# The planner of a two-layer diffusion transformer on one core: matmul durations refitted, and a resource shared by DVE and GpSimd added

## The chip, the cores and the metric

The kernel runs on one core of one Trainium2 chip. The metric is the time on the device, in microseconds (us), of one execution of the whole program; the median of three runs before the change is 2145.59 us. The engines are called as the profile calls them: PE multiplies matrices (PEld is its loading of weights), DVE, ACT and POOL are the vector, scalar and GpSimd engines, and SP issues the DMAs.

## The reference

Two layers work on 256 latent tokens and 256 context tokens of 1024 features. Each layer is a half-step FFN, a token mixer (retention beside latent attention) and a second half-step FFN; a modulation by a condition vector goes ahead of each.

```
mod = (silu_c @ w_ada[l] + b_ada[l])[:, None, :]
mod_c = (silu_cc @ w_ada[l] + b_ada[l])[None, None, :]
...
x = x + 0.5 * g1 * swiglu(modulate(rmsnorm(x), sh1, sc1), ffn1_w1[l], ffn1_w3[l], ffn1_w2[l])
xc = xc + 0.5 * cg1 * swiglu(modulate(rmsnorm(xc), csh1, csc1), ffn1_w1[l], ffn1_w3[l], ffn1_w2[l])
o_lat, o_ctx = token_mixer(...)
x = x + g2 * o_lat
x = x + 0.5 * g3 * swiglu(modulate(rmsnorm(x), sh3, sc3), ffn2_w1[l], ffn2_w3[l], ffn2_w2[l])
```

Here `modulate(h, shift, scale)` is `h * (1 + scale) + shift` and `swiglu` is `(silu(h @ w1) * (h @ w3)) @ w2`. Retention multiplies queries and keys of 8 heads, weights the scores by a decay, multiplies them by the values, normalises each head's output by its mean and variance, and gates it by `silu(g_raw)`. The context has no output in the second layer.

## The kernel before

All features lie on partitions, so each activation is 8 tiles of 128 x 512 (256 latent and 256 context tokens). A matrix product in full precision is made of three products of rounded parts: a value is the sum of a rounded part `hi` and the rest `lo`, and PE does hi by hi, lo by hi and hi by lo (`mm3`). ACT casts a chunk of weights to `wh`, and DVE subtracts it from the raw chunk to get `wl`. For the retention's queries and keys ACT and DVE cast and DVE and POOL subtract (`ret_split`).

The kernel doesn't fix the order of the instructions by hand. The program first records every instruction with the tiles that it reads and writes as a node of a `Plan`. `Plan.order()` then plays through the nodes: each engine takes, of those nodes whose inputs it believes to be ready, the one with the lowest place in the program, corrected by `ahead(n)` for urgent ones. How long a node lasts comes from the table in `Engine.cost()`; how long another engine needs to see its end comes from `LAG`. Tiles have a limited number of slots by kind (51 of `t`, 14 of `u`, 4 each of `raw`, `wh` and `wl`, and 4 each of `m` and `a` in PSUM), and a node with a new tile waits for a slot. `emit()` then issues the instructions in the order found, on the engines' queues. On the chip each engine follows its queue strictly in that order, and waits where an input or a slot is late. All instructions but those of SP are on line 363 for that reason (line 368 in the changed kernel), so tiles tell them apart, not lines.

Three stages matter here. They are called by their stretch of the span.

- The start (0 to 80 us, function `start`). Feature tile by feature tile (k = 0 to 7) the kernel makes the first modulation. For k = 4 to 7 DVE multiplies a row block of the modulation's weights with the row of c and sums it (`junk`, two for each k); POOL makes the same products for the context's row (into `wl`), and ACT sums them. Two tiny instructions (`mod`, 128x2) follow, then the hidden input `H[k]` for each half of the tokens: DVE's `u`, ACT's rounded part, DVE's rest. PE multiplies it with two parts of the first FFN's weights of 128x384, i = 0 and i = 1, that ACT and DVE split as well (`t<-t,t` 128x384): for each k six groups of three products of 512 columns, nine products with i = 0 and nine with i = 1. `ada_stage` and `hidden` are recorded `ahead(URGENT)`, `split` and the products aren't.
- Retention of layer 0 (about 605 to 700 us): `ret_split`, `masks`, `ret_scores` (`a<-t,t` 128x256), `ret_av`, the normalising, and beside them the products of the gates, `g_step` (`m<-t,wh` and `m<-t,wl`, 24 products of 512 columns for each chunk), which need nothing of retention.
- Retention of layer 1 (about 1780 to 1850 us), the same for 256 tokens.

Of the kernel before, what the change touches and what calls it, by code (L numbers as in the profile page):

```python
# [13 lines left out]
F32R = mybir.dt.float32r  # L14
# [4 lines left out]
P = 128  # L19
# [9 lines left out]
# quadrant of a head's rotary rows, and of its unused rows, by head % 4  # L29
# [31 lines left out]
class Halves:  # L61
    """Columns that lie in tiles of their own."""
# [10 lines left out]
class Buffer:  # L73
    """A tile in one of the slots of its kind, from its first instruction to its last one."""
# [15 lines left out]
class View:  # L90
    """A part of a buffer; taken of the tile itself when the instruction is emitted."""
# [23 lines left out]
    def rearrange(self, pattern, **sizes):  # L115
        """Splits and permutes the dimensions after the first."""
# [43 lines left out]
class Node:  # L160
    """Instructions that follow one another on one engine."""

    __slots__ = ("calls", "engine", "cost", "table", "prio", "index", "waits", "after", "bufs", "new", "ready", "start", "end")

    def __init__(self, engine, prio, index):
        self.engine, self.prio, self.index = engine, prio, index
        self.calls, self.cost, self.table = [], 0.0, None
        self.waits, self.after, self.bufs, self.new = set(), [], {}, []
        self.ready, self.start, self.end = 0.0, None, None


class Plan:
    """Takes instructions in the order of the program, and emits them in the order in which engines
    that always take the first of those that are ready would start them."""

    # about how many ns an engine sees it after another is through with an instruction
# [4 lines left out]
    # until when the tensor engine runs at half its speed  # L181
# [13 lines left out]
    @contextmanager  # L195
    def together(self):
        """The instructions of one engine in here are not parted."""
        self.block = False
        yield
        self.block = None  # L200

    @contextmanager
    def ahead(self, n):
        """The instructions in here go before others of up to n places earlier."""
        self.shift += n
        yield
        self.shift -= n

    @contextmanager
    def behind(self, node):  # L210
        """The instructions in here wait for that one."""
        self.held.append(node)
        yield
        self.held.pop()

    def add(self, engine, call, args, kwargs, writes, reads, cost, table):
# [10 lines left out]
        node.table = table  # L227
        for v in reads + writes:
            b = v.buf
            node.waits.update(n for w, n in b.wrote if w.overlaps(v))  # L230
            if b.kind in ("m", "a") and b.wrote:
                # a bank's products come in order, and no reading while there are more to come
# [15 lines left out]
    def order(self):  # L248
# [8 lines left out]
        # free slots, and the indices at which buffers of a kind not yet there come up  # L257
# [8 lines left out]
        dma, table = 0.0, None  # L266
# [5 lines left out]
        def room(n, now):  # L272
            """None where the node's new buffers have slots; else the kind that lacks, and when to look again."""
# [13 lines left out]
        while len(done) < len(nodes):  # L287
# [16 lines left out]
            if e != "PE" and n.cost > self.LONG:  # L304
                # not a long instruction where a far more urgent one comes shortly
# [21 lines left out]
            else:  # L327
                if n.table not in (None, table):
                    now, table = now + self.TABLE, n.table
                slow = 2.0 if e == "PE" and now < self.COLD else 1.0  # L330
# [22 lines left out]
    def emit(self):  # L353
        resolve = lambda v: v.get() if isinstance(v, View) else v  # noqa: E731
# [12 lines left out]
class Engine:  # L367
    """Records the instructions of one engine."""
# [4 lines left out]
    def __getattr__(self, method):  # L373
        call = getattr(self.real, method)

        def record(*args, **kwargs):
# [5 lines left out]
            # the activation functions of one table, which takes its time to load  # L382
            table = {AF.Silu: 0, AF.Exp: 1, AF.Tanh: 1}.get(args[2]) if method == "activation" else None
            return self.plan.add(self.name, call, args, kwargs, out, reads, self.cost(method, out, reads, kwargs), table)

        return record

    def cost(self, method, out, reads, kwargs):
        """About how many ns the engine is held."""
# [6 lines left out]
        if self.name == "PE":  # L396
# [3 lines left out]
            passes = 1 if reads[0].buf.dt == F32R else 4  # L400
# [18 lines left out]
def kernel(  # L419
# [100 lines left out]
    def decays():  # L520
        act.activation(nlg, decT, AF.Exp)
        dve.tensor_scalar(out=lg, in0=nlg, scalar1=-1.0, scalar2=None, op0=ALU.mult)
        # of the two heads of a tile, and of the keys of the context in both directions
# [80 lines left out]
    class Norm:  # L604
        """Root mean square over features, which lie on partitions."""

        def __init__(self, n_tiles, apart=False):
            """apart: the last tile's squares are not added to the others, but come to the sums by themselves."""
# [20 lines left out]
        def stats(self, a, n):  # L629
            """The sums of tokens a..a + n, tokens on partitions."""  # L630
# [13 lines left out]
        def spread(self, a, n):  # L644
            """1 / rms of these tokens on all partitions."""
# [14 lines left out]
    def make_h(y, pair, l, m_sh, k, a):  # L660
        """pair at a = split of y * (1 + scale) + shift."""
# [8 lines left out]
    def modulated(nrm, H, l, m_sh, a, n):  # L670
        """H at a..a + n = split of x / rms * (1 + scale) + shift."""
# [22 lines left out]
    def ada_steps(l, m):  # L694
        """A part of the modulation, its features on partitions: products with the rows of c and c_ctx, summed along the
        rows, by the vector engine for c, by GpSimd and the scalar engine for c_ctx."""
# [26 lines left out]
    def last_gate():  # L723
        """The modulation's last part, wholly on the tensor engine, for a time when that has little else to do."""
# [57 lines left out]
    def update_x(nrm, l, m_g, m, ps, a, b):  # L782
        """x += gate * ps, over tokens a..b, and what the next norm needs of it."""
# [10 lines left out]
    def tail(Ws, X, ks, nrm, l, m_g, n_tok):  # L794
        """The last feature tiles of a residual update: one half of the tokens, then the other one,
        with the first half's norm amid it."""
# [13 lines left out]
    def staggered(nrm, H, l, m_sh, n_tok, groups):  # L810
        """The first products of a phase, half by half as their input comes in.
        groups: pairs of weights, the number of tokens, and what to do with a half of their products."""
# [35 lines left out]
    def ffn(l, w1, w3, w2, m_sh, m_g, nrm_in, nrm_out, n_tok, n_next, fill, pre=None):  # L848
        """pre: hidden input and gated tiles that are there already."""
# [42 lines left out]
        for pi, (k0, k1) in enumerate(PARTS):  # L892
            if pre and pi == 1:
                step(late_consts)
            # at the start more tiles come first, as the gate takes its time
# [29 lines left out]
    def rope(src, cos, sin, mask):  # L925
        """Returns a, b of which the sum is the rotated src (128 x 256, in SBUF)."""
# [8 lines left out]
    def mixer(l, nrm_in, nrm_out, full):  # L935
# [129 lines left out]
        # retention queries and keys, two heads a tile  # L1065
# [12 lines left out]
        # retention values, tokens on partitions  # L1078
# [124 lines left out]
        # a head's keys as (hi; lo) over all rows, its queries' hi and lo twice each: the whole product in two passes  # L1203
        KS, QS = {}, {}
        # for the latent queries and the context's keys: both directions' decayed queries and states, one over the other
# [258 lines left out]
    def start():  # L1464
# [26 lines left out]
        # the rows of c and c_ctx on all partitions  # L1491
# [228 lines left out]
```

## Time and profile before

| what | value |
|---|---|
| runs | 2144.06, 2145.59, 2147.37 us; median 2145.59 |
| span of the profiled execution | 2143.6 us |
| PE busy | 2111.1 us, 98% of the span |
| DVE, ACT, POOL busy | 1419.2, 752.7 and 169.0 us |

The profiled execution's span is 2.0 us under the median of the runs, so what lies around it is taken as 2.0 us. The end of a matmul is modelled in the profile, so that short gaps on PE hide in its busy time; where PE waits is read from its timeline and its granted clock, not from the 98%.

### The profile page before, as it was taken

What the parts mean: (1) busy time and instruction counts of PE and PEld (TensorE: products, weight loads), DVE (VectorE), ACT (ScalarE), POOL (GpSimd) and SP (SyncE); (2) the same over time, 40 slices, a digit from 0 to 9 for tenths busy, and PEclk for the clock granted to TensorE, in tenths of its full rate; (3) what the DMA queues carried; (4) which work ended last, traced back from release to release, by engine and by line L of the source; (5) the groups of instructions that cost most, each with busy time, mean ns of one, the idle gap of its engine ahead of it and who ended that gap; (6) DMA issues with size and microseconds to landing.
All of it is one profiled execution on the core that took longest, in us unless ns stands there. A gap on an engine that the chain in (4) does not pass through costs nothing.

```text
span 2143.6 us, 29821 instructions
## 1 busy us (share of the span) xinstructions
PE 2111.1 (98%) x11610; PEld 1797.2 (84%) x11610; DVE 1419.2 (66%) x2591; ACT 752.7 (35%) x1240; POOL 169.0 (8%) x180
## 2 busy tenths in 40 slices
PE   8999999999999999999999999999999999999998
PEld 5788888987788888988888898888889878999998
DVE  7898885668679435898865473433347977766665
ACT  4422222466433223422212242222225744444433
POOL 3000000211132000100000010000002112100000
PEclk9999999999999999999999999999999999999999
DMA  8476664322212333467666432333333312574663
GB/s 307 130 213 206 199 194 138 87 84 60 63 58 67 107 119 108 120 205 216 191 197 191 128 111 77 108 98 90 98 96 97 116 60 79 155 261 148 204 186 110
DMA packets 86782, 293.76 MB, mean 137 GB/s; under 512 B 9585, under 2 KB 12785, under 8 KB 86641
## 3 DMA queue, kind: packets, MB, share of 16 engines
q1 hardware_dynamic: 86642, 291.87, 44.7%
q8 instruction: 91, 1.49, 0.3%
q14 instruction: 49, 0.40, 0.1%
HBM read 290.78 MB, written 1.05 MB: 136 GB/s over the span
## 4 chain that ended last, share of the span: by engine, by line
PE 83%; DVE 9%; issue 6%; POOL 1%; ACT 1%; DMA 0%; POOLq 0%; DVEq 0%; ACTq 0%
PE m L363 78%; PE a L363 5%; DVE t L363 5%; DVE u L363 2%; DVE wl L363 1%; DVE s L363 1%; DVE junk L363 1%; POOL s L363 1%; ACT t L363 0%; ACT wh L363 0%; POOL t L363 0%; DMA raw<-in_w1b_dram 0%; ACT u L363 0%; DVE x L363 0%; DVE mod L363 0%
## 5 line engine op out<-in xcount | busy, mean ns | idle before, releaser
L363 PE MATMUL m<-t,wh 128*128 128x512 f32 (+1 forms) x6248 | 1643.0, 350 | 0.7 <-DVE t L363 0.6
L363 PEld LDWEIGHTS m<-t,wh 128*128 128x128 f32 x6248 | 1092.1, 188 | 169.0 <-issue 1.9
L363 PE MATMUL m<-t,wl 128*128 128x512 f32 (+1 forms) x3124 | 1085.7, 349 | 0.0
L363 ACT CAST wh<-raw 128x1024 fp32r<-128x1024 f32 (+1 forms) x398 | 408.9, 1029 | 956.5 <-PE m L363 833.9
L363 DVE TENSOR_TENSOR wl<-raw,wh 128x1024 fp32r<-128x1024 f32 (+1 forms) x398 | 477.0, 1199 | 289.2 <-ACT wh L363 288.5
L363 PEld LDWEIGHTS m<-t,wl 128*128 128x128 f32 x3124 | 588.8, 188 | 80.4
L363 DVE SCALAR_TENSOR_TENSOR junk<-raw,crow 128x1024 f32<-128x1024 f32 x220 | 270.6, 1230 | 39.7 <-DMA raw<-in_w_ada_dram 37.5
L363 DVE SCALAR_TENSOR_TENSOR x<-m,mod,x 128x256 f32<-128x256 f32 x192 | 86.5, 480 | 136.7 <-PE m L363 136.5
L363 ACT ACTIVATE t<-m 128x512 f32<-128x512 f32 (+1 forms) x155 | 79.4, 513 | 238.8 <-PE m L363 235.4
L363 DVE TENSOR_TENSOR t<-t,t 128x512 fp32r<-128x512 f32 (+7 forms) x252 | 150.0, 602 | 3.8 <-ACT t L363 1.1
L363 DVE TENSOR_TENSOR t<-t,m 128x512 f32<-128x512 f32 (+1 forms) x91 | 54.5, 599 | 134.2 <-PE m L363 127.4
L363 POOL TENSOR_TENSOR s<-s,mhalf 128x2 f32<-128x2 f32 (+1 forms) x31 | 34.7, 1124 | 1177.0 <-DVE s L363 1176.8
L363 PE MATMUL a<-t,t 128*64 128x256 f32 (+3 forms) x512 | 89.7, 354 | 10.0 <-DVE t L363 7.8
L363 PE MATMUL m<-wh,t 128*128 128x512 f32 x288 | 91.9, 398 | 0.0
L363 PEld LDWEIGHTS a<-t,t 128*128 128x128 f32 (+1 forms) x512 | 66.6, 177 | 29.8 <-DVE t L363 7.8
L363 PE MATMUL m<-t,t 128*128 128x256 f32 (+1 forms) x480 | 75.9, 310 | 8.9 <-ACT t L363 7.4
L363 PEld LDWEIGHTS m<-t,t 128*128 128x128 f32 x480 | 65.3, 191 | 16.2 <-ACT t L363 8.3
L363 PEld LDWEIGHTS m<-wh,t 128*128 128x128 f32 x288 | 53.3, 188 | 12.8 <-issue 1.2
L363 ACT CAST t<-t 128x512 fp32r<-128x512 f32 (+4 forms) x112 | 55.6, 525 | 12.7 <-DVE t L363 11.9
L363 PE MATMUL m<-wl,t 128*128 128x512 f32 x144 | 57.1, 397 | 0.0
L363 ACT ACTIVATE t<-u,mod 128x256 fp32r<-128x256 f32 x88 | 40.1, 500 | 43.0 <-DVE u L363 42.6
L363 POOL MEMSET t<- 32x512 f32 x32 | 16.3, 528 | 431.5 <-PE m L363 217.5
(109 smaller groups left out, 1077.4 us busy)
## 6 DMA issues: line engine op xcount, KB each, us to landing
raw<-in_w_ada_dram SPq DMA_DIRECT2D x124, 512.0 KB, 4.2
raw<-in_w_m_dram SPq DMA_DIRECT2D x76, 512.0 KB, 3.6
raw<-in_w1b_dram SPq DMA_DIRECT2D x44, 512.0 KB, 3.9
raw<-in_w3b_dram SPq DMA_DIRECT2D x44, 512.0 KB, 3.9
raw<-in_w1a_dram SPq DMA_DIRECT2D x41, 512.0 KB, 3.6
raw<-in_w3a_dram SPq DMA_DIRECT2D x41, 512.0 KB, 3.6
raw<-in_w2a_dram SPq DMA_DIRECT2D x32, 512.0 KB, 3.5
raw<-in_w2b_dram SPq DMA_DIRECT2D x32, 512.0 KB, 4.2
```

What stands on the lines that cost most here:

```text
L363: call(*[resolve(v) for v in args], **{k: resolve(v) for k, v in kwargs.items()})
```

## The change

The change touches only what the planner believes. First, a rounded matmul with 128 rows is now costed at columns / 2.25 + 4.3 ns: 231.9 ns for 512 columns, where it was 216.0, and 118.1 ns for 256, where it was 109.4. Second, a node can hold a `port`: every POOL instruction but a memset, and those DVE instructions without a PSUM operand that read two large operands, or are a copy or a tensor_scalar with more than 8 output columns. In the plan such nodes follow one another, whichever of the two engines they are on. All the other lines of the diff only blank comments.

```diff
@@ class Node
-    __slots__ = ("calls", "engine", "cost", "table", "prio", "index", "waits", "after", "bufs", "new", "ready", "start", "end")
+    __slots__ = ("calls", "engine", "cost", "table", "port", "prio", "index", "waits", "after", "bufs", "new", "ready", "start", "end")
...
@@ Plan.add
+        node.port = node.port or port
...
@@ Plan.order
-        dma, table = 0.0, None
+        dma, table, port = 0.0, None, 0.0
...
+                if n.port:
+
+                    now = max(now, port)
+                    port = now + n.cost
                 slow = 2.0 if e == "PE" and now < self.COLD else 1.0
                 n.end = clock[e] = now + slow * n.cost
...
@@ Engine
+    def port(self, method, out, reads, kwargs):
+
+        if self.name == "POOL":
+            return method != "memset"
+        if self.name != "DVE" or any(v.buf.kind in ("m", "a") for v in out + reads):
+            return False
+        big = [v for v in reads if math.prod(v.shape[1:]) > 1]
+        return len(big) > 1 or (method in ("tensor_copy", "tensor_scalar") and math.prod(out[0].shape[1:]) > 8)
...
@@ Engine.cost
-            passes = 1 if reads[0].buf.dt == F32R else 4
+            single = reads[0].buf.dt == F32R
+            passes = 1 if single else 4
+            if single and rows == P:
+                return cols / 2.25 + 4.3
```

No instruction is added or removed. What differs is the order on the engines' queues and the slots of tiles. Of 2345 nodes of DVE 282 stand three or more places off, of 4396 of PE 261, of 1179 of ACT 64, of 171 of POOL 4, and of SP none.

On DVE at the start, before. The rows are those after the junk sums of k = 5 have begun; `t_557` is the rest of the weights' part i = 1 for k = 4, `u_559`, `u_564` and `t_586` make the hidden input of k = 4 (`x_71`):

```order
L363 SCALAR_TENSOR_TENSOR junk,s_522<-raw_363,crow 128x1024
L363 TENSOR_SCALAR mod_1_94<-s_474,sm 128x2
L363 TENSOR_TENSOR t_557<-t_349,t_520 128x384
L363 SCALAR_TENSOR_TENSOR u_559<-x_71,mod_1_94,u_278 128x256
L363 SCALAR_TENSOR_TENSOR u_564<-x_71,mod_1_94,u_287 128x256
L363 TENSOR_SCALAR mod_0_93<-s_522,sm 128x2
L363 SCALAR_TENSOR_TENSOR junk,s_572<-wh_387,crow 128x1024
L363 SCALAR_TENSOR_TENSOR t_586<-u_559,mod_0_93,t_566 128x256
L363 SCALAR_TENSOR_TENSOR t_586<-u_564,mod_0_93,t_566 128x256
```

And on DVE in the changed order, where `t_654` is that same rest for k = 4, i = 1, and `u_637`, `u_641` and `t_647` make the hidden input of k = 6 (`x_73`):

```order
L368 SCALAR_TENSOR_TENSOR u_637<-x_73,mod_1_94,u_289 128x256
L368 SCALAR_TENSOR_TENSOR u_641<-x_73,mod_1_94,u_295 128x256
L368 SCALAR_TENSOR_TENSOR junk,s_589<-wh_422,crow 128x1024
L368 SCALAR_TENSOR_TENSOR t_647<-u_637,mod_0_93,t_644 128x256
L368 SCALAR_TENSOR_TENSOR t_647<-u_641,mod_0_93,t_644 128x256
L368 TENSOR_SCALAR mod_1_94<-s_589,sm 128x2
L368 TENSOR_SCALAR mod_0_93<-s_589,sm 128x2
L368 TENSOR_TENSOR t_654<-t_353,t_496 128x384
L368 SCALAR_TENSOR_TENSOR u_656<-x_74,mod_1_94,u_289 128x256
```

The rest of the weights for k = 4, i = 1 stood ahead of the hidden input of k = 4; it now stands behind the hidden inputs of k = 4, 5 and 6 and all `junk` sums to k = 7. Those for k = 5, 6 and 7 stand behind it.

On PE at the start, before: among the products of k = 4 (`t_566` and `t_586` are its hidden input) those with the part i = 1 (`t_520`, `t_557`) come second:

```order
L363 MATMUL m_369<-t_566,t_520 128x512
L363 MATMUL m_369<-t_566,t_557 128x512
L363 MATMUL m_369<-t_586,t_520 128x512
L363 MATMUL m_397<-t_566,t_517 128x512
L363 MATMUL m_397<-t_566,t_535 128x512
L363 MATMUL m_397<-t_586,t_517 128x512
```

And on PE now (`t_599` and `t_602` are the hidden input of k = 4, `t_491` and `t_575` the part i = 0, `t_496` and `t_654` the part i = 1):

```order
L368 MATMUL a_431<-t_599,t_491 128x512
L368 MATMUL a_431<-t_599,t_575 128x512
L368 MATMUL a_431<-t_602,t_491 128x512
L368 MATMUL m_367<-t_599,t_496 128x512
L368 MATMUL m_367<-t_599,t_654 128x512
L368 MATMUL m_367<-t_602,t_496 128x512
```

All nine products of k = 4 with i = 0 now come first, and the first of i = 1 stand at the row with `t_654`.

On DVE in retention of layer 0, before. `t_5465`, `t_5490` and `t_5492` are pieces of `ret_split` for the next pair of heads, and `BN_STATS` begins the normalising of the last pair's output `a_5495`:

```order
L363 TENSOR_TENSOR t_5447<-t_4706,t_5447 64x512
L363 CAST t_5456<-t_4155 64x512
L363 TENSOR_TENSOR t_5465<-t_4155,t_5456 64x512
L363 TENSOR_TENSOR t_5492<-t_4155,t_5437 64x256 x2
L363 TENSOR_TENSOR t_5479<-t_4706,t_5479 64x512
L363 CAST t_5490<-t_4155 64x512
L363 TENSOR_TENSOR t_5492<-t_4155,t_5437 64x256
L363 TENSOR_TENSOR wl_5513<-raw_5303,wh_5499 128x1024
L363 SCALAR_TENSOR_TENSOR t_5508<-t_5508,m_5422 128x512
L363 BN_STATS s_5531<-a_5495 128x6
```

And the same place now:

```order
L368 TENSOR_TENSOR t_5449<-t_4706,t_5449 64x512
L368 CAST t_5456<-t_4151 64x512
L368 TENSOR_TENSOR wl_5506<-raw_5302,wh_5491 128x1024
L368 SCALAR_TENSOR_TENSOR t_5499<-t_5499,m_5422 128x512
L368 BN_STATS s_5526<-a_5488 128x6
L368 BN_STATS s_5529<-a_5488 128x6
L368 BN_AGGR s_5532<-s_5526 128x2
```

The statistics of the last pair now come ahead of six instructions of `ret_split`.

On PE in retention of layer 0, before. `a_5609` and `a_5616` are scores of the first and the second head of a pair, `m_5623` a product of `g_step`:

```order
L363 MATMUL a_5609<-t_5456,t_5447 128x256
L363 MATMUL a_5609<-t_5465,t_5447 128x256
L363 MATMUL a_5616<-t_5490,t_5479 128x256
L363 MATMUL a_5616<-t_5523,t_5479 128x256
L363 MATMUL a_5616<-t_5490,t_5479 128x256
L363 MATMUL a_5616<-t_5523,t_5479 128x256
L363 MATMUL m_5623<-t_3232,wh_5348 128x512
L363 MATMUL m_5623<-t_3232,wl_5355 128x512
L363 MATMUL m_5623<-t_3245,wh_5348 128x512
```

And the same place now (`a_5602` is the first head's scores, `m_5607` the product of `g_step`):

```order
L368 MATMUL a_5602<-t_5465,t_5449 128x256
L368 MATMUL a_5602<-t_5456,t_5449 128x256
L368 MATMUL a_5602<-t_5465,t_5449 128x256
L368 MATMUL m_5607<-t_3205,wh_5348 128x512
L368 MATMUL m_5607<-t_3205,wl_5355 128x512
L368 MATMUL m_5607<-t_3215,wh_5348 128x512
L368 MATMUL m_5607<-t_3211,wh_5348 128x512
L368 MATMUL m_5607<-t_3211,wl_5355 128x512
L368 MATMUL m_5607<-t_3243,wh_5348 128x512
```

Twelve products of `g_step` now come between the scores of the first and those of the second head, where there were none; later in the stage the same holds at each pair of heads.

## Rows read from the trace of the kernel before

**Rows 1.** The page: busy time of each engine, and the chain that ended last, by engine.

```profile
PE 2111.1 (98%) x11610; PEld 1797.2 (84%) x11610; DVE 1419.2 (66%) x2591; ACT 752.7 (35%) x1240; POOL 169.0 (8%) x180
...
PE 83%; DVE 9%; issue 6%; POOL 1%; ACT 1%; DMA 0%; POOLq 0%; DVEq 0%; ACTq 0%
```

**Rows 2.** Windows, an FFN stage: busy PE PEld DVE ACT POOL (instructions), PEclk, DMA, GB/s.

```profile
1100.00:1200.00 100.00, 100.00 (x433) 80.95 (x432) 55.02 (x81) 21.65 (x26) 0.00 (x0) 1.00 0.60 181
```

**Rows 3.** Windows, the start: the same columns.

```profile
45.00:50.00 5.00, 1.57 (x7) 0.95 (x5) 5.00 (x4) 1.02 (x2) 5.00 (x2) 1.00 0.40 117
50.00:55.00 5.00, 1.04 (x2) 0.50 (x2) 5.00 (x11) 2.00 (x5) 0.82 (x1) 0.65 0.38 105
```

**Rows 4.** Timeline of PE, the start: start, us, instruction, [idle before <- releaser].

```profile
53.96 1.22 PE L363 MATMUL m<-t,t 128*128 128x512 f32 x2 [7.39 <-ACT t L363]
55.43 3.89 PE L363 MATMUL m<-t,t 128*128 128x512 f32 x10 [0.24 <-DVE t L363]
...
70.21 2.92 PE L363 MATMUL m<-t,t 128*128 128x512 f32 x12
...
74.33 0.40 PE L363 MATMUL m<-t,wh 128*128 128x512 f32 x1
```

**Rows 5.** Timeline of DVE, the start.

```profile
39.51 0.33 DVE L363 TENSOR_SCALAR mod<-a,sm 128x2 f32<-128x2 f32 x2
39.77 0.86 DVE L363 SCALAR_TENSOR_TENSOR u<-x,mod,u 128x256 f32<-128x256 f32 x2
40.56 1.21 DVE L363 SCALAR_TENSOR_TENSOR junk<-raw,crow 128x1024 f32<-128x1024 f32 x1
...
41.70 0.87 DVE L363 SCALAR_TENSOR_TENSOR t<-u,mod,t 128x256 fp32r<-128x256 f32 x2
42.50 2.37 DVE L363 TENSOR_SCALAR mod<-s,sm 128x2 f32<-128x2 f32 x1
...
45.93 2.70 DVE L363 TENSOR_TENSOR t<-t,t 128x384 fp32r<-128x384 f32 x1
48.55 3.35 DVE L363 SCALAR_TENSOR_TENSOR junk<-raw,crow 128x1024 f32<-128x1024 f32 x1
...
55.30 3.40 DVE L363 SCALAR_TENSOR_TENSOR junk<-wh,crow 128x1024 f32<-128x1024 f32 x1
```

**Rows 6.** Timeline of POOL, the start.

```profile
42.36 8.46 POOL L363 TENSOR_TENSOR wl<-wh,crow 128x1024 f32<-128x1024 f32 x3 [5.14 <-ACT wl L363]
55.03 2.59 POOL L363 TENSOR_TENSOR wl<-wh,crow 128x1024 f32<-128x1024 f32 x1 [4.21 <-ACT wl L363]
```

**Rows 7.** Windows, retention of layer 0.

```profile
620.00:630.00 10.00, 6.98 (x33) 5.91 (x32) 8.49 (x27) 2.43 (x4) 2.02 (x2) 0.75 0.19 55
```

**Rows 8.** Timeline of PE, retention of layer 0.

```profile
620.51 0.72 PE L363 MATMUL a<-t,t 128*128 128x256 f32 x4
622.85 0.71 PE L363 MATMUL a<-t,t 128*128 128x256 f32 x4 [1.62 <-DVE s L363]
...
625.66 2.93 PE L363 MATMUL a<-t,t 128*128 128x128 f32 x12 [1.40 <-DVE t L363]
...
635.26 0.63 PE L363 MATMUL m<-t,wh 128*128 128x512 f32 x2
...
650.40 0.59 PE L363 MATMUL a<-t,t 128*128 128x256 f32 x3 [1.06 <-DVE t L363]
...
655.33 1.04 PE L363 MATMUL a<-ident,t 128*128 128x128 f32 x8
```

**Rows 9.** Timeline of DVE, retention of layer 0.

```profile
610.46 1.23 DVE L363 CAST t<-t 64x512 fp32r<-64x512 f32 x1
...
623.91 1.36 DVE L363 TENSOR_SCALAR t<-a,s,s 128x128 f32<-128x128 f32 x4 [1.12 <-POOL s L363]
```

**Rows 10.** Timeline of PE, retention of layer 1.

```profile
1800.23 0.49 PE L363 MATMUL a<-t,t 128*128 128x128 f32 x2 [2.66 <-DVE t L363]
```

**Rows 11.** Windows, retention of layer 1.

```profile
1800.00:1810.00 10.00, 9.77 (x85) 9.77 (x85) 10.00 (x30) 4.32 (x11) 1.94 (x3) 1.00 0.34 107
```

More of the change, by code (lines that the diff above doesn't have):

```diff
@@ L160 @@
 class Node:
-    __slots__ = ("calls", "engine", "cost", "table", "prio", "index", "waits", "after", "bufs", "new", "ready", "start", "end")
+    __slots__ = ("calls", "engine", "cost", "table", "port", "prio", "index", "waits", "after", "bufs", "new", "ready", "start", "end")
     def __init__(self, engine, prio, index):
         self.engine, self.prio, self.index = engine, prio, index
-        self.calls, self.cost, self.table = [], 0.0, None
+        self.calls, self.cost, self.table, self.port = [], 0.0, None, False
         self.waits, self.after, self.bufs, self.new = set(), [], {}, []
@@ L214, in behind, with add @@
         self.held.pop()
-    def add(self, engine, call, args, kwargs, writes, reads, cost, table):
+    def add(self, engine, call, args, kwargs, writes, reads, cost, table, port):
         if self.block:
@@ L383, in record @@
             table = {AF.Silu: 0, AF.Exp: 1, AF.Tanh: 1}.get(args[2]) if method == "activation" else None
-            return self.plan.add(self.name, call, args, kwargs, out, reads, self.cost(method, out, reads, kwargs), table)
-        return record
+            return self.plan.add(self.name, call, args, kwargs, out, reads, self.cost(method, out, reads, kwargs), table,
+                                 self.port(method, out, reads, kwargs))
+        return record
+    def port(self, method, out, reads, kwargs):
[5 more added lines that the diff above has]
+        return len(big) > 1 or (method in ("tensor_copy", "tensor_scalar") and math.prod(out[0].shape[1:]) > 8)
     def cost(self, method, out, reads, kwargs):
```

## The prediction

> **What bounds the kernel now.** I read the page first: PE is busy 98% of the span and carries 83% of the chain that ended last, DVE 9% [rows 1]. The windows then say what PE's pace is where it waits for nothing: in an FFN stage 433 products of 512 columns take 100 us, 0.231 us each, at full clock [rows 2]. Such a stage can't be shortened by another order. So only stages where PE waits can gain, and what PE loses anywhere is lost for good. The windows by short stretches show where it waits: at the start (1.57 us busy of 5 from 45 us, 1.04 from 50 us, with a granted clock of 0.65) [rows 3], in retention of layer 0 (6.98 of 10 from 620 us, granted clock 0.75) [rows 7] and in retention of layer 1 (9.77 of 10 from 1800 us, behind a wait that ended there) [rows 10, 11]. In all three DVE is the busy one: 5.00 of 5, 8.49 of 10, 10.00 of 10.
>
> The timelines give the waits themselves. At the start PE waits 7.39 us for the first half of the hidden input of k = 4, until 53.96, and then runs with small gaps to the first FFN product at 74.33 [rows 4]. In layer 0 it waits 1.62 and 1.40 us near 623 and 625 and 1.06 at 650 [rows 8]; in layer 1 2.66 us at 1800 [rows 10].
>
> The reason for the new resource is visible too. POOL's products 5 to 8 run from 42.36 for 8.46 us and from 55.03 for 2.59 [rows 6]. In just these stretches four DVE instructions are held: 2.37 us for a 128x2 tensor_scalar, of which two take 0.26 together elsewhere (39.51 to 39.77); 2.70 for a 128x384 subtraction; 3.35 and 3.40 for a junk sum that takes 1.14 (40.56 to 41.70) [rows 5]. DVE loses some 2.2 us at each, 8.9 us in all.
>
> **The change, part by part.** No instruction comes or goes, so all of it is order.
>
> *The start: a loss.* The rests of the weights with i = 1 have moved behind the hidden inputs of k = 4, 5 and 6. PE meets them in order: after nine products of k = 4 with i = 0 it must wait for that of k = 4, i = 1, and everything else of the start stands behind it. When does DVE come to it? From 39.77 on the changed order has ahead of it 16 scalar_tensor_tensor of 128x256 (two take 0.79, 39.77 to 40.56), 7 junk sums at 1.14, 8 tensor_scalar of 128x2 at 0.13 and one 128x384 subtraction. For the last, nothing free of POOL is among the rows; by its columns between a 128x256 and a 128x1024 instruction I estimate 0.5. That is 6.3 + 8.0 + 1.0 + 0.5 = 15.8 us, so 55.6 without any hold-up. POOL's products 5 to 8 still fall into this stretch, as the same four are needed for the sums. They held DVE for 8.9 us before [rows 5], and each engine still takes its own queue without regard to the other; I take the same, so DVE begins at 64.5, and PE goes on at about 65.2 (0.5 for the instruction and 0.2 to be seen, by the 0.24 us that PE waited for DVE at 55.43 [rows 4]). Bounds: one hold-up fewer (62.3, PE at 63.0), or one more of 2.2 (PE at 67.4). After that PE has 9 + 3 x 18 = 63 products, at 0.231 us 14.6 us, and the first FFN product stands at 79.8 instead of 74.33: +5.5, between +3.3 and +7.7.
>
> The Trainium skill, "SBUF — State Buffer" (Who interferes with whom), has a rule that speaks against the new resource: whichever of DVE and GpSimd issues first holds the shared ports for its whole instruction, and the other blocks. By it an order planned over two queues doesn't prevent a hold, and all four would stay, which makes the same 5.5. The trace shows the holds; it doesn't show that a plan can avoid them.
>
> The clock comes on top. The 12 products from 53.96 are busy for 1.22 + 3.89 = 5.1 us [rows 4], where 12 x 0.231 is 2.8: after the wait of 7.39 us the clock was half, 1.2 GHz (0.65 on average from 50 to 55 [rows 3]), which cost some 2.2 us. In the changed kernel there are two waits, one for the hidden input of k = 4 as before and a new one of some 6 us. The second may cost these 2.2 again, or nothing; a wait of 1.62 us in layer 0 [rows 8] also stands in a stretch with a low clock [rows 7], so I take half, 1.1. Start: **+6.6, from +3.3 to +9.9**.
>
> The Trainium skill, "TensorE: Matmul & The Clock Gate" (Part 1), says the same of the clock: it is throttled by default, and an idle stretch throttles it again to half. By that rule alone the second wait would cost the full amount, and the sum would be 1.1 us higher. The trace agrees for the wait of 7.39 us; no row here shows a single wait of 6 us.
>
> *Retention of layer 0: a gain.* Here DVE takes the statistics and the normalising ahead of `ret_split`, and PE has twelve products of `g_step` between the scores of the first and second head. Before, PE went from 620.51, where it began the first head's scores, to about 635.5 (the second product group at 635.26 + 0.23) for 15.0 us of span [rows 8]. The work in it is 21 products of `g_step` (21 x 0.231 = 4.9), 16 score products of 256 columns (half of 0.231 each, 1.9), and 16 products of 128 columns at most 0.13 each (8 take 1.04, row of 655.33), 2.1: together 8.9. So 6.1 us are waits and half clock. Afterwards the first twelve `g_step` products (2.8 us) cover the time until DVE has the second head's rests. DVE reaches those at: end of the cast that begins at 610.46 (some 1.2 us, 611.7 [rows 9]), and then in the changed order `wl`, the gate's product, two sets of statistics, two normalisings and six pieces of `ret_split`; before, the same work was done at 625.3 (623.91 + 1.36), with 1.12 us of waiting for POOL in it [rows 9], which `ret_split` now fills. So I take 622.5 to 624; PE comes there at 620.5 + 0.5 + 2.8 = 623.8. That is tight, but at most some tenths. Later the wait of 1.06 at 650 goes for the same reason, and some tenths more. DVE, busy 8.49 of 10 there, gets free sooner as well, since its waits for PE shrink. Upper bound 6.1 + 1.06 + 1.3 (my estimate for smaller gaps that the modelled ends hide) = 8.5; lower 5.5, if PE comes 0.6 too early for the second head and waits as long at 650 as before. I take **-7.2**.
>
> *Retention of layer 1: nearly nothing.* The wait of 2.66 us at 1800 is for DVE, and fillers now come ahead of it. But DVE has 10.00 of 10 us from 1800 to 1810 [rows 11] and its work is the same: PE uses up products of `g_step` early and lacks them at the later scores. I take **-0.5**, from -2.7 (that wait goes and none comes back) to +1.
>
> *Elsewhere.* Neighbours are swapped at the beginning of the mixer and FFN phases and in latent attention, 1.5 us either way at most by the sizes of the waits there (none over that of rows 8); taken as 0. The refitted matmul cost agrees with the trace, 231.9 ns against 0.231 us [rows 2], but by itself it moves no time.
>
> *Sum.* 2143.6 + 6.6 - 7.2 - 0.5 = 2142.5 of span, and 2.0 around it: **2144.5 us**, 1.1 below the median of 2145.59.
>
> **The rivals.** I count 0.2% (4.3 us) as what a measurement can tell from no change.
>
> *Faster.* The start loses only its lower bound, +3.3, because POOL's products come earlier in the new order and hold DVE three times instead of four; layer 0 gives -8.0 and layer 1 -2.0. Sum -6.7: 2138.9. For it: POOL waited 5.14 and 4.21 us for ACT before its products [rows 6], and ACT's sums now stand further ahead. Against it: ACT's queue then has them ahead of the rounded parts of k = 3 and 4. Chance 0.29.
>
> *Slower.* The start costs the full +9.9: one more hold-up and half clock after the second wait. Then layer 0 decides it: if its gain is 5.5 or more, the time stays within 4.4 of before; if the early use of the `g_step` products leaves PE without work at the last pair of heads, as I expect of layer 1, only -3 stays. Sum about +6: 2152. It needs DVE to come later than some 624 to the second head's rests. Chance 0.24.
>
> *Nothing much moves.* PE is fixed by data, the order of a few instructions of DVE is worth below 2 us everywhere, start included. For it: PE is 98% busy. Against it: the wait of 7.39 us is real and the new one is plain in the queue. 2145.6. Chance 0.1.
>
> **How the numbers follow.** My forecast (a loss at the start and about the same gain in layer 0) has 0.37, with its own range of 2141 to 2149.5. With the third rival, within 0.2% has 0.47; faster 0.29, slower 0.24. The range reaches from the faster case, a little beyond (2138), to the slower (2152).
>
> **What would show it.** The first FFN product (`m<-t,wh`) of the start at 79.8 to 82 instead of 74.33, with a wait of PE of some 6 us near 60 for a 128x384 subtraction. The windows of 620 to 640 with PE near full, allowing for the shift, and no wait above 0.5 us before the end of that stage. A wait in layer 1 of about the same sum as before. I am wrong if DVE gets to `t_654` before 60, if the start doesn't move, or if PE waits again at the later pairs of layer 0.

## The result, and the profile after

The changed kernel takes 2162.4 us (median of 4 runs, 2159.01 to 2166.87), the kernel before 2145.69 on the same chip (four runs now): the ratio is 1.0079, 95% interval [1.0067, 1.0091]. The forecast of 2144.5 us, and its range up to 2152, were wrong: the kernel became slower by some 17 us. Its profiled execution has a span of 2156.9 us, 13.3 more than before; it is the shortest of the four runs, so some 3 us of the median's difference are not in this trace.

The page of the changed kernel: span, busy time, and the chain that ended last, by engine and by line.

```profile
span 2156.9 us, 29805 instructions
...
PE 2117.0 (98%) x11610; PEld 1801.8 (84%) x11610; DVE 1416.3 (66%) x2591; ACT 752.9 (35%) x1240; POOL 168.7 (8%) x180
...
PE 75%; DVE 10%; issue 8%; DMA 5%; POOL 1%; ACT 1%; SPq 0%; POOLq 0%; DVEq 0%; ACTq 0%
PE m L368 69%; PE a L368 6%; DMA raw<-in_w_ada_dram 5%; DVE junk L368 4%; DVE t L368 3%; DVE wl L368 2%; DVE u L368 1%; DVE s L368 1%; ACT t L368 0%; DVE x L368 0%; POOL t L368 0%; POOL s L368 0%; DMA x<-in_xT_dram 0%; DMA raw<-in_w2a_dram 0%; SPq L368 0%
```

PE is as busy as in [rows 1], with 6 us more in its column (2117.0). What is new stands in the chain: DMA has 5% of it, where it had 0% before, by the weights of the modulation (`raw<-in_w_ada_dram`), and the `junk` sums that read them have 4%, where they had 1%. PE's share fell from 83 to 75%. So the chain now runs through DMAs that bring weights of the modulation, and nothing in the forecast had these. A share of the chain isn't time lost; what these DMAs cost is measured below.

To find the places I set the start of each PE instruction in this trace against that of the same instruction in the trace of before. The lag is 10.4 us at the end of the start, constant to 230 us; 16.8 from 250 us on; 9.1 at 700 us, after layer 0's retention; 10.4 at 900 and 11.2 at 1100 us; 10.6 before and 13.4 behind layer 1's retention. So: start +10.4, first FFN +6.4, retention of layer 0 -7.8, later FFN stages some +2, retention of layer 1 +2.7.

**The start.** Windows (columns as in [rows 2]), then PE's timeline and DVE's, of the changed kernel:

```profile
60.00:65.00 5.00, 2.49 (x6) 1.39 (x5) 5.00 (x14) 3.45 (x5) 0.00 (x0) 0.74 0.22 77
65.00:70.00 5.00, 2.07 (x5) 1.69 (x6) 5.00 (x14) 3.26 (x6) 0.00 (x0) 0.60 0.00 0
70.00:75.00 5.00, 5.00 (x18) 3.92 (x17) 5.00 (x8) 0.00 (x0) 0.00 (x0) 0.71 0.15 18
```

```profile
41.16 1.01 PE L368 MATMUL a<-sel,u 128*128 128x2 f32 x4 [4.39 <-ACT u L368]
...
57.54 0.72 PE L368 MATMUL m<-t,t 128*128 128x512 f32 x2 [2.62 <-ACT t L368]
...
67.93 2.50 PE L368 MATMUL m<-t,t 128*128 128x512 f32 x5 [5.44 <-DVE t L368]
...
84.72 0.40 PE L368 MATMUL m<-t,wh 128*128 128x512 f32 x1
```

```profile
42.80 3.00 DVE L368 SCALAR_TENSOR_TENSOR u<-x,mod,u 128x256 f32<-128x256 f32 x2
45.72 5.18 DVE L368 SCALAR_TENSOR_TENSOR t<-u,mod,t 128x256 fp32r<-128x256 f32 x2
50.82 3.44 DVE L368 SCALAR_TENSOR_TENSOR junk<-raw,crow 128x1024 f32<-128x1024 f32 x1
...
67.33 0.54 DVE L368 TENSOR_TENSOR t<-t,t 128x384 fp32r<-128x384 f32 x1
```

PE waits 4.39 us at 41 us, 2.62 for the hidden input of k = 4 and then 5.44, until 67.93, for the 128x384 subtraction that DVE begins at 67.33. That is the new wait of the forecast, for the instruction that it named. From 67.93 to the first FFN product at 84.72 there are 62 products (the first of the forecast's 63 stands ahead of the wait, at 61.86); they take 16.8 us, where 62 at 0.231 take 14.3. The granted clock is 0.74, 0.60 and 0.71, partly half speed. DVE's holds are there as before: 3.00 and 5.18 us for pairs that take 0.79, 3.44 for a junk sum of 1.14, together 8.9 us beyond these, the same as in [rows 5].

But the first `u` of k = 3, at 42.80, is already 3 us late; it began at 39.77 [rows 5]. The delay begins at k = 1, whose modulation DVE made at 22.98 before, and now here:

```profile
26.98 0.34 DVE L368 TENSOR_SCALAR mod<-a,sm 128x2 f32<-128x2 f32 x2 [3.13 <-PE a L368]
```

PE's granted clock is 0.50 from 15 to 25 us in this trace (0.76 and 1.00 before). POOL's first four products, from 27.74, then hold DVE at k = 1, and all of k = 2 comes behind them.

**The first FFN.** DVE's timeline at the gate of one chunk before, the same in the changed kernel, and then PE's timeline there:

```profile
230.31 0.69 DVE L363 TENSOR_TENSOR t<-t,m 128x512 f32<-128x512 f32 x1 [1.16 <-PE m L363]
231.03 0.43 DVE L363 CAST t<-t 128x512 fp32r<-128x512 f32 x1
...
232.54 0.68 DVE L363 TENSOR_TENSOR t<-t,t 128x512 fp32r<-128x512 f32 x1
233.14 1.22 DVE L363 SCALAR_TENSOR_TENSOR junk<-raw,crow 128x1024 f32<-128x1024 f32 x1
```

```profile
232.65 0.68 DVE L368 TENSOR_TENSOR t<-t,m 128x512 f32<-128x512 f32 x1
236.46 1.22 DVE L368 SCALAR_TENSOR_TENSOR junk<-raw,crow 128x1024 f32<-128x1024 f32 x1 [3.13 <-DMA raw<-in_w_ada_dram]
...
237.61 0.42 DVE L368 CAST t<-t 128x512 fp32r<-128x512 f32 x1
237.95 1.22 DVE L368 TENSOR_TENSOR wl<-raw,wh 128x1024 fp32r<-128x1024 f32 x1
239.08 0.68 DVE L368 TENSOR_TENSOR t<-t,t 128x512 fp32r<-128x512 f32 x1
...
247.56 1.22 DVE L368 SCALAR_TENSOR_TENSOR junk<-raw,crow 128x1024 f32<-128x1024 f32 x1 [1.95 <-DMA raw<-in_w_ada_dram]
...
250.18 0.68 DVE L368 TENSOR_TENSOR t<-t,t 128x512 fp32r<-128x512 f32 x1
```

```profile
249.19 0.50 PE L368 MATMUL m<-t,wh 128*128 128x512 f32 x1 [3.62 <-DVE t L368]
...
250.92 1.22 PE L368 MATMUL m<-t,wh 128*128 128x512 f32 x2 [1.01 <-DVE t L368]
```

Before, the junk sum stood behind the gated tile's rounding (CAST) and rest (`t<-t,t`). Now it stands ahead of them: DVE has the gated product (`t<-t,m`) at 232.65, then waits 3.13 us, and at the next chunk again 1.95, for a DMA of `in_w_ada`, at a junk sum. Right behind it in DVE's queue stand the CAST, the rest of a weight chunk (`wl`) and the rest of the gated tile, which PE needs for its next products: PE waits 3.62 and 1.01 us. Its granted clock is 0.66 from 250 to 255 us, so the rest of the 6.4 us lies in products at half speed. From 75 to 400 us PE waits for nothing in the trace of before. DVE's waits for these DMAs in the whole stretch of 100 to 400 us, before and after (us in total, times, longest):

```profile
DVE junk L363 <- DMA raw<-in_w_ada_dram: 9.4, 13, 1.8
```

```profile
DVE junk L368 <- DMA raw<-in_w_ada_dram: 24.2, 20, 3.1
```

And from 900 to 1250 us (the second FFN of layer 0 nearly all of it), where PE has no wait in the trace of before either:

```profile
DVE junk L363 <- DMA raw<-in_w_ada_dram: 17.2, 11, 2.6
```

```profile
DVE junk L368 <- DMA raw<-in_w_ada_dram: 51.8, 31, 3.3
```

These DMAs wait for DVE in turn, which frees their slots: waits of SP's queue from 180 to 250 us in the changed kernel:

```profile
SPq L368 <- DVE wl L368: 24.5, 10, 6.0
SPq L368 <- DVE junk L368: 22.2, 12, 2.5
```

Before they were as large in total, 29.6 and 22.6 us, though the longest was 3.4. The median time to landing of these DMAs is 4.2 us in both pages. So the DMAs didn't become slower; DVE comes to their sums at another place of its queue.

**Retention.** Windows of layer 0 in the changed kernel, then of layer 1 in the kernel before and in the changed one:

```profile
620.00:630.00 10.00, 10.00 (x66) 8.94 (x65) 9.76 (x17) 6.02 (x12) 4.95 (x5) 1.00 0.18 54
...
660.00:670.00 10.00, 9.18 (x55) 7.86 (x54) 9.85 (x24) 2.54 (x5) 0.17 (x1) 1.00 0.20 54
```

```profile
1830.00:1840.00 10.00, 8.67 (x72) 8.14 (x71) 9.89 (x25) 4.22 (x9) 1.08 (x2) 1.00 0.21 61
1840.00:1850.00 10.00, 10.00 (x87) 10.00 (x86) 9.38 (x23) 4.26 (x7) 1.93 (x1) 1.00 0.72 219
```

```profile
1830.00:1840.00 10.00, 8.86 (x78) 8.65 (x76) 9.38 (x27) 5.11 (x11) 4.61 (x6) 1.00 0.29 93
1840.00:1850.00 10.00, 7.18 (x29) 6.43 (x30) 7.96 (x19) 2.26 (x7) 1.27 (x2) 0.55 0.16 52
```

And PE's waits in layer 1 of the changed kernel, from 1780 to 1865 us:

```profile
PE m L368 <- DVE t L368: 2.7, 2, 1.4
PE a L368 <- ACT t L368: 1.5, 1, 1.5
PE a L368 <- DVE t L368: 1.2, 2, 0.7
```

In layer 0, where the clock was 0.75 with 6.98 us busy of 10 [rows 7], PE now runs through at full clock but for one short stretch (one wait of 0.8 us for DVE). In layer 1 the waits have moved back by some 20 us; their sum, 5.4 us, is near that of before (4.8), but the clock falls to 0.55, where it was 1.00 in every window of the stage before.

### The profile page after: what moved, and what is told of

It reads as the page before. It is cut to its first block, busy times and chain, and to the rows that moved or that the text cites. A ratio compares the mean times of both kernels' runs of the same rounds, so it can differ in the third digit from the quotient of the medians.

```text
span 2156.9 us, 29805 instructions
## 1 busy us (share of the span) xinstructions
PE 2117.0 (98%) x11610; PEld 1801.8 (84%) x11610; DVE 1416.3 (66%) x2591; ACT 752.9 (35%) x1240; POOL 168.7 (8%) x180
## 4 chain that ended last, share of the span: by engine, by line
PE 75%; DVE 10%; issue 8%; DMA 5%; POOL 1%; ACT 1%; SPq 0%; POOLq 0%; DVEq 0%; ACTq 0%
PE m L368 69%; PE a L368 6%; DMA raw<-in_w_ada_dram 5%; DVE junk L368 4%; DVE t L368 3%; DVE wl L368 2%; DVE u L368 1%; DVE s L368 1%; ACT t L368 0%; DVE x L368 0%; POOL t L368 0%; POOL s L368 0%; DMA x<-in_xT_dram 0%; DMA raw<-in_w2a_dram 0%; SPq L368 0%
```

## The experiments

Each part of the change can be switched by itself, and by the node's place in the program. The queues of all other stages keep their order.

**The matmul costs alone** (`refit_only`). The resource is recorded, but not used in the plan:

```diff
-                if n.port:
-                    now = max(now, port)
-                    port = now + n.cost
```

> Only the matmul costs are refitted, the planner has no shared resource. On DVE the order of 100 to 260 us and 950 to 1100 us moves as in the changed kernel (junk sums ahead of gate instructions), the start doesn't. Theory 1 (the refit pulls junk sums, which wait for their DMA, ahead of the gate of the first FFN): the wait of some 6.4 us of PE near 235 to 250 us is here, the start ends with the first FFN product at 74.3 as before, layer 0's retention stays as long as before; about 2152 us, +6. Rival (that wait is a result of the late start or of this one execution): no wait there, about 2146.

Measured: 2171.88 us, ratio 1.0121 [1.0106, 1.0136]. Theory 1 holds for the first FFN (the lag rises by 6.0 us near 240) and the rival falls. But the refit alone does far more harm than I expected, some 26 us: some 4.6 near 1085 us, some 5 in layer 1's mixer, and layer 0's retention isn't as before but loses 6 us. Why it harms the retention stages when it is alone wasn't tested. PE's waits of 600 to 700 us in that run (us in total, times, longest), where they were 1.62, 1.40 and 1.06 us before [rows 8]:

```profile
PE a L364 <- DVE t L364: 8.1, 7, 2.6
```

**The resource alone** (`port_only`):

```diff
-            if single and rows == P:
-                return cols / 2.25 + 4.3
```

> Only the shared resource, with the old matmul costs. Theory 1: the start loses about 10.4 us (first FFN product near 84.7), no wait of PE from 100 to 400 us, retention of layer 0 gains about 7.8, retention of layer 1 loses about 2.7; sum +5.3, about 2151 us. Rival (the wait near 240 us follows from the late start): it is here too, about 2157. Second rival (the gain of layer 0 needs the refit): layer 0 as before, about 2159.

Measured: 2149.65 us, ratio 1.0014 [1.0004, 1.0024]. No wait of PE from 100 to 400 us, so both rivals fall, and layer 0 gains without the refit. The lag is 12.3 us behind the start, 3.3 behind layer 0's retention, 5 from 900 us on and 6.0 at the end. Its profiled run is the longest of its ten.

**The changed kernel without the resource at the start** (`port_not_start`):

```diff
-                if n.port:
+                if n.port and n.index > 374:
```

> The changed kernel, but the shared resource counts only for nodes recorded after the start. All queues are those of the changed kernel except up to about 80 us, where they are nearly those of before. Theory 1: the start's 10.4 us come back, the wait near 240 stays (6.4), so about 2152 us. Rival (the wait near 240 is a result of the late start): it goes too, about 2146.

Measured: 2153.24 us (2147.59 to 2155.52, 10 runs), ratio 1.0031 [1.0021, 1.004]. The start's loss comes back and the step of the lag near 240 us stays (5.4 us), as theory 1 says. Its runs lie 7.9 us apart; the 19 runs of the kernel before beside it lie 5.7 apart.

**The resource at the start alone** (`port_start_only`, `n.port and n.index < 375`, old matmul costs):

> The kernel before, but the shared resource counts for the nodes of the start alone. Theory 1: +10.4 us and nothing else, about 2156 us, PE waits near 41, 57 and 62 to 68 us. Rival (the start's loss is partly given back, as DMAs run ahead meanwhile): less than +5. Rival (the late start brings the wait near 240): +17, about 2162.

Measured: 2154.95 us, ratio 1.0041 [1.0026, 1.0056], 8.8 us. The start's loss is the resource's, and from 100 to 400 us PE has no wait.

**The resource in the second half of the start** (`port_start_late`, `n.port and 230 < n.index < 375`):

> The kernel before, but the shared resource counts only in the second half of the start (from the hidden input of k = 3 on). On DVE the order of the start is that of the changed kernel, with the splits of the weights behind the hidden inputs; on PE the swap of two neighbours near 22 us is not there. Theory 1a (the splits that come late are most of the loss, as predicted): +5 to +7, about 2152. Rival 1b (the swap near 22 us makes k = 1 to 3 late and is most of it): +2 or less, about 2148. If the swap costs nothing: +9, about 2155.

Measured: 2154.42 us, ratio 1.0039 [1.0026, 1.0053], 8.4 us. Without the swap on PE near 22 us the loss is the same, so rival 1b falls. This doesn't price the swap, though: k = 1 is in time here (23.49), but POOL's fifth product follows the fourth at once, at 38.17, where it waited 5.14 us before, until 42.36 [rows 6]. It holds DVE for 3.22 us at a pair of subtractions that took 1.01:

```profile
38.41 3.22 DVE L368 TENSOR_TENSOR t<-t,t 128x384 fp32r<-128x384 f32 x2
```

So the first `u` of k = 3 begins at 42.96, as late as in the changed kernel by another way. PE's timeline, at the wait and at the first FFN product:

```profile
67.33 2.50 PE L368 MATMUL m<-t,t 128*128 128x512 f32 x5 [5.22 <-DVE t L368]
...
83.59 0.40 PE L368 MATMUL m<-t,wh 128*128 128x512 f32 x1
```

**The splits of the start's weights as urgent** (`start_splits_urgent`, on top of `port_start_only`):

```diff
-            split(k)
+            with plan.ahead(URGENT):
+                split(k)
```

> The kernel with the resource in the start alone, and the splits of the start's weights recorded as urgent: the rest for k = 4, i = 1 stands at the 58th place of DVE instead of the 82nd (60th before), the swap on PE near 22 us stays. Theory 1a: 5 to 7 us of the start's 9 to 10 come back, about 2149. Rival 1b (the swap is most of it): about 2154.

Measured: 2146.17 us, ratio 1.0002 [0.9993, 1.0011]: all of the loss comes back, more than the 5 to 7 us expected. PE's timeline at the same places:

```profile
73.33 2.60 PE L368 MATMUL m<-t,t 128*128 128x512 f32 x10 [0.59 <-DVE t L368]
...
77.17 0.40 PE L368 MATMUL m<-t,wh 128*128 128x512 f32 x1
```

The wait of 5.2 us and the half clock behind it are gone. By the times the late rests of the weights are the whole of the start's loss, within the interval; by this trace they are most of it, as 77.17 is still 2.8 us behind the 74.33 of before.

**Junk sums that don't wait** (`no_ada_wait`: every queue as in the changed kernel, first FFN only):

```diff
+                    if n.other is not None:
+                        kwargs = dict(kwargs, in0=n.other)
...
+                    if len(plan.nodes) < 1300:
+                        plan.nodes[-1].other = crow[:, 1024:2048]
```

> All queues as in the changed kernel, but the junk sums of the first FFN (to about 390 us) read a tile that is there already instead of the weights that their DMA brings; the modulation's values from these sums are left out. The DMAs are still issued. Theory 1 (junk sums at the head of DVE's queue wait for their DMA, and the gate behind them makes PE wait): no wait of PE from 225 to 275 us, some 6 us less than the changed kernel, about 2156. Rival (DVE simply has too much to do ahead of the gate): the wait stays, about 2162.

Measured: 2157.53 us, ratio 1.0055 [1.0041, 1.0068]: 5.2 us less by the ratios than the changed kernel. PE has no wait from 225 to 275 us, and all waits of DVE from 100 to 275 us are now for other things:

```profile
DVE t L370 <- PE m L370: 12.0, 8, 2.8
DVE x L370 <- PE m L370: 7.0, 5, 2.4
DVE wl L370 <- ACT wh L370: 5.6, 9, 2.0
```

**The same in all stages** (`no_ada_wait_all`):

> All queues as in the changed kernel, but every junk sum after the start reads a tile that is there already, in the later FFN stages too; the modulation's values from these sums are left out. Theory 1 (the refit's whole price is junk sums that wait for their DMA at the head of DVE's queue, also near 900 and 1075 us, and their DMAs come earlier or later from run to run): some 5 us less than with the first FFN alone, about 2152, with runs within 3 us of each other. Rival (the losses after 900 us have another cause): about 2157.

Measured: 2151.49 us (2151.27 to 2152.74, 7 runs), ratio 1.0029 [1.0017, 1.004]. Another 5.6 us go. The order is unchanged, and what was taken away is DVE's wait for the DMA, with SP's waits for these sums; so 10.7 us (1.0079 against 1.0029) are its price. The kernel before wasn't run with this edit, but PE has no wait in its trace from 75 to 400 and from 900 to 1250 us, so there was nothing to gain in these stretches. The spread goes as well: 1.5 us between 7 runs, where the changed kernel has 7.9 between 4. With the first FFN's waits alone gone it was 1.6 between 4 already. That the DMAs make the difference between runs is likely by this, but the longest runs left no trace.

**The refit in the first FFN alone** (`refit_ffn1`, `single and rows == P and len(self.plan.nodes) < 1300`):

> The kernel before, with the refitted matmul costs in the start and the first FFN of layer 0 alone (to about 390 us). Theory 1 (the refit alone pulls junk sums ahead of the gate): +6 us, about 2152, PE waits near 235 to 250 us. Rival (it needs the late start or the later refit): about 2146 to 2147.

Measured: 2152.18 us (2148.61 to 2152.82, 8 runs), ratio 1.0024 [1.0014, 1.0035], 5.2 us. It needs neither the late start nor the later refit: set against the trace of before, nearly all DVE instructions that stand three or more places off (25 of 27) lie between 100 and 260 us. DVE's waits from 100 to 275 us, and PE's from 225 to 275:

```profile
DVE junk L364 <- DMA raw<-in_w_ada_dram: 20.8, 12, 3.2
```

```profile
PE m L364 <- DVE t L364: 4.5, 2, 4.0
```

**The resource in layer 0's mixer alone** (`port_mixer0`, `n.port and 1360 < n.index < 3200`, old matmul costs):

> The kernel before, but the shared resource counts for the nodes of layer 0's token mixer alone; matmul costs as before. Its queues from 600 to 700 us are those of the run with the resource alone, all others those of before. Theory 1 (the gain of layer 0 comes from the resource in that stage: statistics ahead of the splits, gate products between the scores): 8 to 9 us faster, about 2137.5, PE without waits from 620 to 690 us. Rival (the gain of that stage only gives back what the late start and the first FFN had lost): no difference, about 2146.

Measured: 2138.31 us, ratio 0.9964 [0.9951, 0.9978], 7.7 us faster than the kernel before: the best version, and theory 1 to within 1 us. Its windows show PE at work all the time and at full clock, which [rows 7] don't:

```profile
620.00:630.00 10.00, 10.00 (x59) 8.65 (x58) 7.90 (x19) 3.02 (x5) 0.57 (x1) 1.00 0.19 54
630.00:640.00 10.00, 10.00 (x70) 9.09 (x68) 9.67 (x33) 4.66 (x9) 3.57 (x3) 1.00 0.15 53
```

**The resource in layer 1's mixer alone** (`port_mixer1`, `n.port and 6000 < n.index < 7360`, old matmul costs):

> The kernel before, but the shared resource counts for the nodes of layer 1's token mixer alone. Theory 1 (there the same rule costs time: gate products are used up early, PE then waits for DVE and its clock falls): +2.5 to +4 us, about 2149. Rival (the loss of layer 1 in the changed kernel comes from its late arrival or from other stages): no difference, about 2146.

Measured: 2147.44 us, ratio 1.0008 [0.9998, 1.0017], between the two theories; the interval holds no difference. In its trace the lag goes from -1.1 us ahead of the mixer to -2.6 at 1790 us and to 1.3 behind the stage, a gain of 1.5 and a loss of 3.9, with the clock at half in nearly all of one window:

```profile
1830.00:1840.00 10.00, 8.01 (x39) 7.58 (x39) 8.00 (x20) 1.96 (x6) 0.00 (x0) 0.54 0.17 54
```

**The changed kernel again** (`changed_again`):

> The changed kernel once more, for a second trace. Theory 1: start and layer 0 as in its first trace within 2 us, and what is longer than there lies where junk sums wait for a DMA (near 240, 900 and 1075 us). Rival: the difference between its runs lies in the start or in retention.

Measured: 2159.91 us, 0.9 more than the first trace's run. The steps of the lag differ from that trace's by +0.5 us in the start, by -1 near 250 us and by +1.3 near 1100 us. So the start differs little and the larger differences lie in the FFN stages, as theory 1 says; but it is also a run at the short end, so the longest runs weren't seen.

## Why the prediction was wrong

**The step that failed** is "The refitted matmul cost agrees with the trace, [...] but by itself it moves no time", with its companion, that an FFN stage "can't be shortened by another order" and so only places where PE waits needed a look. The first is false: by itself the refit cost 26 us (`refit_only`). The second is only half of it: a stage where PE doesn't wait can't gain, but it can lose. A planner that believes PE slower believes that more time has gone by when a DMA is needed. It therefore finds the weights of the modulation "there" sooner, seen from PE's place, and puts the junk sums ahead of the CAST and the subtraction of the gate. On the chip a slot of `raw` comes free only when DVE has done with it, SP waits for that, and the DMA then takes 4.2 us in the median; DVE stands at the junk sum, and the gate behind it is late. The refit was nearer to PE's true pace (231.9 ns against 231) and made the plan worse. The wait at these sums costs 10.7 us in the changed kernel (`no_ada_wait_all`), 5.2 of these in the first FFN (`no_ada_wait`, `refit_ffn1`). The forecast had the moved nodes counted by engine; by stretch, 102 of DVE's instructions between 100 and 260 us stand at another place in the two traces, 25 of them three or more places off, in a stage that the forecast took as fixed. Why the planner moved them is argued from its code; that the moved sums' wait is the price is shown.

**The start**: the mechanism was right, the size near the upper bound by times and past it in the trace. Forecast was +6.6 (+3.3 to +9.9); measured 8.8 by times (`port_start_only`), 10.4 in the trace, and 8.8 to 12.3 in the other traces with DVE in this order. DVE came to the instruction at 67.33 instead of 64.5, with holds of 8.9 us as forecast: the first `u` of k = 3 begins at 42.80, where it began at 39.77, 3 us that I had taken as unmoved. The traces show two ways to these 3 us: in the changed kernel k = 1 comes late and then meets POOL's first products, in `port_start_late` POOL's fifth product comes early (there DVE begins the instruction at 66.73). The forecast priced neither. The half clock then came a second time and in full: 16.8 - 14.3 = 2.5 us, of which I had taken 1.1; my count of 63 products was one too many. The Trainium skill, "TensorE: Matmul & The Clock Gate" (Part 1), says that an idle stretch throttles the clock again; here the trace agrees, with 0.60 in the window in which the wait of 5.44 us ends. The Trainium skill, "SBUF — State Buffer" (Who interferes with whom), says that whoever issues first holds the shared ports for its whole instruction; the trace agrees there too: although the plan keeps the two engines apart, DVE was held for the same 8.9 us.

**Retention of layer 0**: right. Forecast -7.2, measured -7.7 (`port_mixer0`) and -7.8 in the trace of the changed kernel. The place and the missing waits are as described, but for one wait of 0.8 us at a later pair of heads. That the resource in this stage is the cause is shown; that it works by the statistics ahead of the splits and the gate products between the scores fits the queues and wasn't tested apart. One caution: kernels whose queues in that stage are those of before ran through it 1.4 to 2.3 us faster than the trace of before (by the lag ahead of it and behind it), so that trace stood at the long end there. The forecast's 6.1 us of waits were read from it, so that it met -7.7 this closely is in part luck.

**Retention of layer 1**: forecast -0.5, bounds -2.7 to +1; the trace of the changed kernel has +2.7, `port_mixer1` +1.7 with an interval that holds zero. The reason given (gate products are used up early and lacking later) fits the trace and wasn't tested, but I had not priced the clock: the waits at the end stand closer together now, and half speed follows. By the trace the loss is past the forecast's bound; by the times it isn't clear of zero.

**The rivals**: the slower one ended on the right side by another mechanism. It needed layer 0 to lose its gain, and layer 0 kept it.

**The sum**: 8.8 - 7.7 + 10.7 + 1.7 = 13.5 us of the 16.9 that 1.0079 makes of 2145.7. About 3 us, the parts' effect on one another included, aren't attributed. The resource's three parts make 2.8, and `port_only` measured 3.0 (1.0014), so these 3 us came with the refit, if they are more than noise: the intervals of `port_only` and `no_ada_wait_all`, between which they lie, overlap.

## What to carry to other kernels

A better number in a planner's table is not a better plan: the refit alone, right about PE, made this kernel some 26 us slower. A refit of one entry can move every place where two engines' clocks are compared; here it was the places of instructions that wait for DMAs on an in-order queue that cost the most in the changed kernel. So read the order of the whole program after such a change, also where nothing waits yet, and ask of each instruction that moved ahead what it waits for and who stands behind it. And switch such a rule by stage: the shared resource was worth 7.7 us in one stage, nothing to speak of in a second, and cost 8.8 in a third.

## What the runs showed of the hardware

In each of the seven traces that have the wait for the late rest at the start (5.2 to 6.9 us), the first five products behind it took 2.50 us, where five at 0.231 take 1.2: half clock. In some of them PE was at half clock before that wait as well (`port_start_late`, 0.50 from 60 to 65 us). `start_splits_urgent` has waits of 2.96 and 1.94 us there, with granted clocks of 0.66 and 0.79 in the windows behind them, and its first FFN product at 77.17, where `port_start_only` has it at 84.80. In layer 1 waits of at most 1.5 us each, close to one another, stand ahead of a granted clock of 0.55 over 10 us.

DVE kept to its queue while it waited: at 236.46 it had stood 3.13 us before a sum whose DMA hadn't landed, with the CAST that PE needed behind it, although the gated product was done at 233.3. With such waits the changed kernel's runs went from 2159 to 2167 us; without them seven runs lay within 1.5 us. Whether the landing times themselves differ from run to run wasn't seen.
